# Three more weight buffers up to the first attention outputs, more halves split in advance, and another load order in the projection, in a one-layer encoder kernel

## The chip, the cores and the metric

The kernel runs on one core of one Trainium2 chip. The metric is the time of one execution on the device in microseconds (us). Where a distribution is given it is the median of the runs, with the lowest and the highest. One further execution was profiled; all views come from it.

## The reference

One layer of an encoder: attention over a window, then an MLP, each with a modulation by a conditioning vector c and a LayerNorm behind it. 256 tokens, width 2048, 32 query heads and 8 key heads of 64, hidden width 8192, everything in float32. Cut to its core:

```python
c_act = silu(c)                                            # 1 x 2048
sh_m, sc_m, g_m, sh_f, sc_f, g_f = split(c_act @ mod_w + mod_b, 6)   # mod_w: 2048 x 12288
h = x * (1 + sc_m) + sh_m                                  # 256 x 2048
q, k, v = split(h @ w_qkv + b_qkv)                         # 2048, 512, 512 columns; rotary on q and k
s = where(|qpos - kpos| <= 128, q k^T / 8, -inf)           # 4 query heads share a key head
m = max(max(s), sink)
p = exp(s - m) / (sum(exp(s - m)) + exp(sink - m))
x = layer_norm(ALPHA * x + (1 + g_m) * ((p v) @ w_o + b_o))
h = x * (1 + sc_f) + sh_f
x = layer_norm(ALPHA * x + (1 + g_f) * (relu(h @ w1 + b1) ** 2 @ w2 + b2))
```

The six modulation vectors need 100 MB of weights, as vector times matrix; w_qkv is 25 MB, w_o 17 MB, w1 and w2 67 MB each.

## The kernel before

**Precision.** A float32 product is made from rounded parts: each operand is split into a high part, rounded to fp32r, and a low part, the rest. Three matmuls (`mm3`: high by high, high by low, low by high) stand for one product. So every weight passes through ScalarE (the cast to `wh`, L234) and DVE (the difference `wl`, L206) before TensorE reads it in L472, L473 and L474.

**The weight stream.** All large weights come through one object, `Stream`, in blocks of 1 MB ([128 x 2048] float32). `plan` appends a block to the list `q`. `loads` (L188) issues the next block's DMA on SyncE's queue whenever one of the five buffers of the pool `raws` (`RAWS = 5`) is free; `self.free` counts them, in program order, and a buffer counts as free as soon as the instructions that read it have been issued. At run time the DMA waits until they have ended. A block has two kinds of use. A matmul block is split in two halves of 1024 columns: `pump` issues the cast of a half into a tile of the pool `whp` and `low` the difference into one of `wlp` (five tiles each); the buffer is counted free after the second half's difference. `S.nh` and `S.nl` say how many halves may be split ahead of the one in use (5 and 5 from the start, 4 and 2 from L604, 5 and 5 again from L835). A modulation block is used in whole, by `Mod.step`.

**Modulation.** `Mod.step` multiplies a block with c_act, either on TensorE (L292, small matmuls into the one bank of the pool `psm`) or, for the blocks that the set `dve` names, on DVE (L329, L331) into partial sums, which one more group of matmuls adds up at the end. `m_mix` are six groups of the attention's scale and shift (of 1, 1, 2, 4, 4, 4 column chunks of 128: `MIXG`), with 2 blocks for each chunk; `m_gm` is the attention's gate (16 blocks; blocks 5, 9, 12, 14 on DVE), `m_ff` the MLP's scale and shift, and `m_gf` the MLP's gate (all on DVE; its bias is added at its last step, L307 to L310).

**The projection.** Input group g is made by `modulated(g)`: the modulation's row is turned into columns, and ScalarE writes x times scale plus shift, rounded (L508), DVE the low part (L509, L510). Then `qkv(g, c)` multiplies chunk c of the group with its block of w_qkv (24 blocks in all, in the stream's order). A block of 4 column chunks has 48 matmuls into two PSUM banks; `evict` adds them into the sums `acc` on DVE (L526) where they aren't held in PSUM for the next block (`CARRY`). `ORDER` is the order of the chunks of a group. The lists in L409 to L425 say how the modulation blocks of group g + 1 lie between the w_qkv blocks of group g in the stream. The last six blocks of w_qkv (`LATE`: the query columns 3 to 5 of groups 4 and 5) come in the attention.

**The attention.** Keys and queries are rotated, split and turned (`split_k`, `split_q`, `heads_T` with its transposes in L677). A loop of 21 steps n (L856) overlaps the stages of 16 blocks of scores: `scores(n)` (L709, L710; exponentials on ScalarE in L723, with row sums), `normalise(n)` (L738), `probs_T(n - 1)` (transposes L748, copies L750), `values`, and between them one block of matmuls as filler: the six late blocks in steps 0 to 3, nothing in step 4, and from step 5 on the output projection `project` with w_o. `SLOT_FILL` says how many blocks of the gate and the MLP's modulation are planned in each step. In step 5 four tiles `ys` begin, at `gate` two more; the MLP takes `ys` anew, with two tiles for the second bias (`bias_all`).

**General tiles.** All other data of [128 x 1024] floats (x, group inputs, sums, keys, queries, probabilities, gate) lies in one pool, `gen`, of 26 tiles (`g4()`). A request for a tile waits until the oldest one that was given back is no longer read.

**Order.** The program is written in loops; a scheduler orders the instructions of each engine by their priority and by what they depend on. In the first part (`S.pin`) the casts, differences and modulation steps are kept in program order, and L508 to L510 always are.

Of the kernel before, what the change touches and what calls it, by code (L numbers as in the profile page):

```python
# [20 lines left out]
S = 256  # L21
# [16 lines left out]
         [(1, 0), (1, 1), (1, 3), (1, 2)]]  # L38
RAWS = 5
NHIGH = 5  # L40
NLOW = 5
# [4 lines left out]
def hybrid_kernel(ctx: ExitStack, tc: tile.TileContext, a, out: bass.AP):  # L46
# [5 lines left out]
    wlp = ctx.enter_context(tc.tile_pool(name="wlp", bufs=NLOW))  # L52
    gen = ctx.enter_context(tc.tile_pool(name="gen", bufs=26))
    psa = ctx.enter_context(tc.tile_pool(name="psa", bufs=5, space=PSUM))
    pst = ctx.enter_context(tc.tile_pool(name="pst", bufs=2, space=PSUM))
    psm = ctx.enter_context(tc.tile_pool(name="psm", bufs=1, space=PSUM))

    def g4(dt=F32):
# [101 lines left out]

    def bias_all(src):

        b = [g4(), g4()]
        for h in range(2):
            nc.gpsimd.dma_start(b[h], src[:, h * 1024:h * 1024 + 1024].partition_broadcast(128))
        return lambda c: b[c // 2][:, (c % 2) * 512:(c % 2) * 512 + 512]


    class Stream:
# [4 lines left out]
        def __init__(self):  # L174
            self.q, self.raw = [], []
            self.hs, self.ls, self.src = [], [], []
            self.free, self.used = RAWS, 0
            self.at = self.im = 0
            self.nh, self.nl = NHIGH, NLOW
            self.stop = 0  # L180
            self.pace = VECS
            self.pin = False
            self.side = {}
# [4 lines left out]
        def loads(self):  # L188
            while len(self.raw) < len(self.q) and self.free:
                if len(self.raw) in self.side:  # L190
                    self.side.pop(len(self.raw))()
                r = raws.tile([128, 2048], F32, name="raw")
                nc.sync.dma_start(r, self.q[len(self.raw)][0])
                self.raw.append(r)
                self.free -= 1

# [5 lines left out]
        def low(self):  # L202
            n = len(self.ls)
            r, kept = self.src[n]
            l = g4(F32R) if kept else wlp.tile([128, 1024], F32R, name="wl")
            self.pinned(nc.vector.tensor_sub(l, r, f32(self.hs[n])))  # L206
            self.ls.append(l)
            self.free += n % 2

        def pump(self, vecs, must=0):  # L210

            while len(self.ls) < must or self.at < len(self.q):
# [9 lines left out]
                if use is not None:  # L222
                    if not vecs and n >= must:
                        return
                    vecs = max(vecs - 1, 0)
                    use(self.raw[self.at])
                    self.at += 1
                    self.free += 1
                    continue
# [5 lines left out]
                self.hs.append(h)  # L235
                self.src.append((s, kept))
                self.at += n % 2

# [16 lines left out]
        def vecs(self, n):  # L255

            for _ in range(n):
                self.loads()
                if self.q[self.at][1] is None:
                    break  # L260
                self.q[self.at][1](self.raw[self.at])
                self.at += 1
                self.free += 1
            self.loads()
# [6 lines left out]
    class Mod:  # L271
# [26 lines left out]
        def step(self, raw):  # L298
# [7 lines left out]
            if last and self.whole:  # L306
                for n, p in enumerate(self.part):  # L307
                    b = g4()
                    nc.gpsimd.dma_start(b[0:1], self.bias[:, n * 1024:(n + 1) * 1024])
                    nc.gpsimd.tensor_add(p[0:1], p[0:1], b[0:1])  # L310
            elif i == self.n - 6 and self.bias is not None:
# [3 lines left out]
            for k in range(kc):  # L315
# [5 lines left out]
                elif i in self.dve:  # L321
                    e = min(4 * w, 1024)
                    new = self.part is None
                    if new:
                        self.part = [g4() for _ in range(4 * w // e)]
                    for n, p in enumerate(self.part):
# [39 lines left out]
    def gate(m):  # L366

        g = [g4(), g4()]
        src = [m.part[j // 2][:, (j % 2) * 512:(j % 2) * 512 + 512] for j in range(4)] if m.whole else [m.r]
# [42 lines left out]
    S.plan(a["wqkv"][1])  # L412
    S.plan(a["wqkv"][2])
    S.side[len(S.q)] = lambda: load_x(1)
    m_mix[2][0].plan(4)
    for g in range(2, G):
        n = len(ORDER[g])
        if g + 1 < G:
            S.side[len(S.q)] = lambda g=g: load_x(g)
        for x, c in enumerate(ORDER[g]):  # L420
            if g + 1 < G:
                m_mix[g + 1][0].plan([0, 0, 2][x] if g == 2 else [1, 2, 2, 1, 2, 0][x] if n == 6 else [3, 3, 2][x])
            wq(g, c)
        if g == 2:
            m_mix[3][0].plan(6)  # L425
    late = [m_gm] + [m[0] for m in m_ff[:3]]
# [176 lines left out]
    msk, pick = masks()  # L603
    S.nh, S.nl = 4, 2  # L604
    S.pace = 1
# [228 lines left out]

    S.nh, S.nl = NHIGH, NLOW  # L835
    kA = whole(rope(4, 0))
    khl = split_k(kA)
# [18 lines left out]
    for n in range(21):  # L856
# [10 lines left out]
        elif n < 5:  # L867
            w = iter((0, 1))
        else:
            if n == 5:  # L870
                ys = [g4() for _ in range(4)]
            w = project((n - 5) // 4, (n - 5) % 4)
# [165 lines left out]

    ys = [g4() for _ in range(4)]
    bf = bias_all(a["b2"])  # L1040
    for blk in range(BLK - 1):
# [140 lines left out]
```

## Time and profile before

| | |
|---|---|
| median of 3 runs | 1133.27 us (1132.55 to 1133.56) |
| profiled execution | 1132.9 us; its span in the profile 1131.2 us |
| TensorE's mean granted clock | 0.988 of full speed |
| TensorE matmuls (PE) | 1093.4 us busy, 97% of the span |
| TensorE weight loads (PEld) | 882.9 us, 78%, beside the matmuls |
| VectorE (DVE) | 808.9 us, 72% |
| ScalarE (ACT) | 545.9 us, 48% |
| GpSimd (POOL) | 28.9 us, 3% |
| DMA | 288.51 MB, mean 255 GB/s |

PE, PEld, DVE, ACT, POOL and SP (SyncE) are the engines. In the profile's forty slices each digit is an engine's busy share in tenths; PEclk is the clock that the throttle granted to TensorE. "L234" is line 234 of the kernel. A group's row has: line, engine, operation, output and input tiles, shapes and count, then busy time and mean ns of one, then the idle time of the engine ahead of these instructions and what ended most of it. A row of the timeline has: start, length, engine, line, operation, and in brackets the engine's idle time before it and what ended that. A row of the waits has: who waited, for what, then the total in us, the number of waits and the longest. A row of DMA issues ends with the median time from issue to landing.

The profile orders the chain of work that ended last by line: PE's L472, L473 and L474 (projections with mm3) have 17% each, L1012 (the MLP's first layer) 16%, DMA as a whole 3%, DVE 2%, ACT 1%.

### The profile page before, as it was taken

How to read it: one execution, taken by the hardware profiler on the slowest of the kernel's cores; microseconds unless marked ns; L12 is line 12 of the kernel's file. 1: busy time of each engine (PE TensorE's matmuls, PEld its weight loads, DVE VectorE, ACT ScalarE, POOL GpSimd, SP SyncE). 2: the span in 40 equal slices, each digit the busy share in tenths (PEclk: the TensorE clock that was granted, in tenths of full speed). 3: DMA queues.
4: the chain of work that ended last, by engine and by line, in shares of the span. 5: the costliest groups of instructions: out<-in, count | busy, mean ns of one | idle time of the engine just before them, and what ended most of it. 6: DMA issues, size and time to landing. Idle time of an engine off the chain costs nothing.

```text
span 1131.2 us, 15803 instructions
## 1 busy us (share of the span) xinstructions
PE 1093.4 (97%) x6258; PEld 882.9 (78%) x6258; DVE 808.9 (72%) x1122; ACT 545.9 (48%) x852; POOL 28.9 (3%) x48
## 2 busy tenths in 40 slices
PE   8779799999999999999999999999999999999995
PEld 6547576666676699998888888888888888888884
DVE  5477887877989977865568888866665656665576
ACT  6313255776676264753444543435444334444340
POOL 2000000000000000000000001020000000000001
PEclk9998999999999999999999999999999999999998
DMA  9799987867886699655577788874555557555521
GB/s 376 320 414 368 376 322 284 335 223 252 315 323 227 226 382 359 230 185 198 203 276 284 264 287 294 313 271 171 186 187 186 192 201 269 188 188 188 189 75 75
DMA packets 42882, 288.51 MB, mean 255 GB/s; under 512 B 5036, under 2 KB 5676, under 8 KB 9016
## 3 DMA queue, kind: packets, MB, share of 16 engines
q1 hardware_dynamic: 39824, 279.85, 67.1%
q0 software_dynamic: 2112, 6.32, 1.8%
q10 hardware_dynamic: 872, 1.34, 0.3%
q8 instruction: 49, 0.80, 0.3%
q14 instruction: 25, 0.20, 0.0%
HBM read 285.39 MB, written 2.10 MB: 254 GB/s over the span
## 4 chain that ended last, share of the span: by engine, by line
PE 93%; DMA 3%; DVE 2%; ACT 1%; issue 1%; DVEq 0%; ACTq 0%
PE pa L472 17%; PE pa L473 17%; PE pa L474 17%; PE pa L1012 16%; PE pa L1013 8%; PE pm L292 4%; PE pa L989 3%; PE pa L988 3%; PE pa L990 3%; DMA raw<-in_wqkv 2%; PE pa L763 2%; PE pt L748 1%; PE pa L709 1%; PE pt L677 1%; PE pa L710 1%; PE pa L590 1%
## 5 line engine op out<-in xcount | busy, mean ns | idle before, releaser
L206 DVE TENSOR_TENSOR wl<-raw,wh 128x1024 fp32r<-128x1024 f32 x332 | 405.6, 1227 | 230.7 <-ACT wh L234 230.2
L234 ACT CAST wh<-raw 128x1024 fp32r<-128x1024 f32 x332 | 347.9, 1053 | 451.7 <-PE pa L474 240.3
L472 PE MATMUL pa<-wh,g 128*128 128x512 f32 x816 | 322.7, 397 | 10.1 <-ACT g L508 8.8
L473 PE MATMUL pa<-wl,g 128*128 128x512 f32 x816 | 320.8, 394 | 1.2 <-DVE wl L206 1.2
L474 PE MATMUL pa<-wh,g 128*128 128x512 f32 x816 | 318.1, 392 | 0.0
L1012 PE MATMUL pa<-g,wh 128*128 128x512 f32 x768 | 271.6, 399 | 0.0
L1013 PE MATMUL pa<-g,wl 128*128 128x256 f32 x768 | 215.7, 281 | 0.0
L472 PEld LDWEIGHTS pa<-wh,g 128*128 128x128 f32 x816 | 154.6, 190 | 50.3 <-ACT g L508 10.8
L473 PEld LDWEIGHTS pa<-wl,g 128*128 128x128 f32 x816 | 154.6, 189 | 34.3 <-issue 1.8
L474 PEld LDWEIGHTS pa<-wh,g 128*128 128x128 f32 x816 | 153.9, 189 | 34.0 <-DVE g L510 0.9
L1012 PEld LDWEIGHTS pa<-g,wh 128*128 128x128 f32 x768 | 144.3, 188 | 35.8
L1013 PEld LDWEIGHTS pa<-g,wl 128*128 128x128 f32 x768 | 145.2, 189 | 0.2
L331 DVE SCALAR_TENSOR_TENSOR g<-raw,cact,g 128x1024 f32<-128x1024 f32 x81 | 103.2, 1279 | 8.0 <-DMA raw<-in_modgf 4.7
L989 PE MATMUL pa<-g,wh 128*128 128x256 f32 x256 | 72.7, 285 | 0.4 <-DVE g L932 0.4
L988 PE MATMUL pa<-g,wh 128*128 128x256 f32 x256 | 72.5, 286 | 0.0
L990 PE MATMUL pa<-g,wl 128*128 128x256 f32 x256 | 72.3, 283 | 0.0
L292 PE MATMUL pm<-raw,cact 128*32 128x256 f32 (+2 forms) x832 | 59.3, 381 | 10.3 <-DMA raw<-in_modm 9.2
L988 PEld LDWEIGHTS pa<-g,wh 128*128 128x128 f32 x256 | 48.8, 192 | 1.3 <-issue 0.8
L989 PEld LDWEIGHTS pa<-g,wh 128*128 128x128 f32 x256 | 49.1, 192 | 0.9 <-DVE g L932 0.8
L990 PEld LDWEIGHTS pa<-g,wl 128*128 128x128 f32 x256 | 49.1, 192 | 0.0
L292 PEld LDWEIGHTS pm<-raw,cact 128*32 128x32 f32 x832 | 22.7, 110 | 32.7 <-issue 11.4
L526 DVE TENSOR_TENSOR g<-g,pa 128x512 f32<-128x512 f32 x42 | 27.7, 681 | 17.4 <-PE pa L474 17.4
(178 smaller groups left out, 812.7 us busy)
## 6 DMA issues: line engine op xcount, KB each, us to landing
raw<-in_w SPq DMA_DIRECT2D x64, 1024.0 KB, 4.9
raw<-in_w1b SPq DMA_DIRECT2D x48, 1024.0 KB, 4.9
raw<-in_modm SPq DMA_DIRECT2D x32, 1024.0 KB, 8.1
raw<-in_modf SPq DMA_DIRECT2D x32, 1024.0 KB, 6.7
raw<-in_wqkv SPq DMA_DIRECT2D x24, 1024.0 KB, 8.1
raw<-in_modgm SPq DMA_DIRECT2D x16, 1024.0 KB, 5.8
raw<-in_wo SPq DMA_DIRECT2D x16, 1024.0 KB, 7.0
raw<-in_w1a SPq DMA_DIRECT2D x16, 1024.0 KB, 6.7
```

The source lines that it names most:

```text
L206: self.pinned(nc.vector.tensor_sub(l, r, f32(self.hs[n])))
L234: self.pinned(nc.scalar.copy(h, s))
L292: i = nc.tensor.matmul(self.ps[32 * j:32 * j + 32, :w], lhsT[j] if type(lhsT) is list else lhsT, rhs[j], start=self.first, stop=stop)
L331: nc.vector.scalar_tensor_tensor(p[:, :e], s, cact[:, kt:kt + 1], p[:, :e], op0=OP.mult, op1=OP.add)
L472: nc.tensor.matmul(ps, xh, wh, start=start, stop=False)
L473: nc.tensor.matmul(ps, xh, wl, start=False, stop=False)
L474: nc.tensor.matmul(ps, xl, wh, start=False, stop=stop)
L988: nc.tensor.matmul(o, wh(w, 128), hh, start=new, stop=False)
L989: nc.tensor.matmul(o, wh(w, 128), hl, start=False, stop=False)
L990: nc.tensor.matmul(o, wl(w, 128), hh, start=False, stop=end)
L1012: nc.tensor.matmul(ps, wh(k, 128), hb, start=k == 0, stop=False)
L1013: nc.tensor.matmul(ps[:, :256], wl(k, 128), hb[:, :256], start=False, stop=k == NK - 1)
```

## The change

- **Buffers.** A second pool, `raws2`, of three 1 MB buffers (`MORE = 3`) stands beside the five of `raws`. `self.free` becomes a list of pools from which `loads` takes the next buffer; `home` remembers where each block lies, and `freed` returns its buffer. From the line after the projection's loop on (`S.deep = False`), buffers of `raws2` are no longer returned.
- **General tiles.** The pool `gen` has 20 tiles instead of 26. The room of `raws2` is given at its first use after that to six tiles `g4b`: `ys` (from step n = 5), the gate's tiles, the MLP's `ys` and its second bias, and the partial sums of the MLP's gate.
- **Halves.** `S.nh, S.nl` are 5, 4 instead of 4, 2 in the projection.
- **Order of loads.** In the projection the last modulation block of group 2 comes after the first w_qkv block of that group; the first w_qkv block of each later group comes at the end of the group before it, one block ahead of the last modulation block for group 3; the modulation blocks lie otherwise between the w_qkv blocks. Blocks and bytes in all are the same.
- **The MLP gate's bias** is loaded and added in four pieces of 512 in the small tiles `t2` instead of two pieces of 1024 in general tiles.

```diff
--- before.py
+++ after.py
@@ -37,6 +37,7 @@
          [(0, 4), (0, 5), (1, 4), (1, 5)],
          [(1, 0), (1, 1), (1, 3), (1, 2)]]
 RAWS = 5
+MORE = 3
 NHIGH = 5
 NLOW = 5
 VECS = 2
@@ -50,10 +51,22 @@
     raws = ctx.enter_context(tc.tile_pool(name="raws", bufs=RAWS))
     whp = ctx.enter_context(tc.tile_pool(name="whp", bufs=NHIGH))
     wlp = ctx.enter_context(tc.tile_pool(name="wlp", bufs=NLOW))
-    gen = ctx.enter_context(tc.tile_pool(name="gen", bufs=26))
+    gen = ctx.enter_context(tc.tile_pool(name="gen", bufs=20))
     psa = ctx.enter_context(tc.tile_pool(name="psa", bufs=5, space=PSUM))
     pst = ctx.enter_context(tc.tile_pool(name="pst", bufs=2, space=PSUM))
     psm = ctx.enter_context(tc.tile_pool(name="psm", bufs=1, space=PSUM))
+
+
+    early = ExitStack()
+    ctx.push(early.__exit__)
+    raws2 = early.enter_context(tc.tile_pool(name="raws2", bufs=MORE))
+    more = []
+
+    def g4b(dt=F32):
+        if not more:
+            early.close()
+            more.append(ctx.enter_context(tc.tile_pool(name="gen2", bufs=2 * MORE)))
+        return more[0].tile([128, 1024], dt, tag="g4b", name="g4b")
 
     def g4(dt=F32):
         return gen.tile([128, 1024], dt, tag="g4", name="g4")
@@ -158,7 +171,7 @@
 
         return add
 
-    def bias_all(src):
+    def bias_all(src, g4=g4):
 
         b = [g4(), g4()]
         for h in range(2):
@@ -174,7 +187,9 @@
         def __init__(self):
             self.q, self.raw = [], []
             self.hs, self.ls, self.src = [], [], []
-            self.free, self.used = RAWS, 0
+            self.free, self.home, self.used = [raws] * RAWS + [raws2] * MORE, [], 0
+            self.of = []
+            self.deep = True
             self.at = self.im = 0
             self.nh, self.nl = NHIGH, NLOW
             self.stop = 0
@@ -189,10 +204,14 @@
             while len(self.raw) < len(self.q) and self.free:
                 if len(self.raw) in self.side:
                     self.side.pop(len(self.raw))()
-                r = raws.tile([128, 2048], F32, name="raw")
+                self.home.append(self.free.pop(0))
+                r = self.home[-1].tile([128, 2048], F32, name="raw")
                 nc.sync.dma_start(r, self.q[len(self.raw)][0])
                 self.raw.append(r)
-                self.free -= 1
+
+        def freed(self, n):
+            if self.deep or self.home[n] is raws:
+                self.free.append(self.home[n])
 
         def pinned(self, i):
 
@@ -205,7 +224,8 @@
             l = g4(F32R) if kept else wlp.tile([128, 1024], F32R, name="wl")
             self.pinned(nc.vector.tensor_sub(l, r, f32(self.hs[n])))
             self.ls.append(l)
-            self.free += n % 2
+            if n % 2:
+                self.freed(self.of[n])
 
         def pump(self, vecs, must=0):
 
@@ -225,7 +245,7 @@
                     vecs = max(vecs - 1, 0)
                     use(self.raw[self.at])
                     self.at += 1
-                    self.free += 1
+                    self.freed(self.at - 1)
                     continue
                 if n >= must and (n - self.used >= self.nh or kept):
                     return
@@ -234,6 +254,7 @@
                 self.pinned(nc.scalar.copy(h, s))
                 self.hs.append(h)
                 self.src.append((s, kept))
+                self.of.append(self.at)
                 self.at += n % 2
 
         def main(self):
@@ -260,7 +281,7 @@
                     break
                 self.q[self.at][1](self.raw[self.at])
                 self.at += 1
-                self.free += 1
+                self.freed(self.at - 1)
             self.loads()
 
     S = Stream()
@@ -304,10 +325,11 @@
             last = self.i == self.n
             per = 1024 // w
             if last and self.whole:
-                for n, p in enumerate(self.part):
-                    b = g4()
-                    nc.gpsimd.dma_start(b[0:1], self.bias[:, n * 1024:(n + 1) * 1024])
-                    nc.gpsimd.tensor_add(p[0:1], p[0:1], b[0:1])
+                for n in range(4):
+                    b, p = sml.tile([128, 512], F32, name="br", tag="t2", bufs=4), self.part[n // 2]
+                    p = p[0:1, n % 2 * 512:n % 2 * 512 + 512]
+                    nc.gpsimd.dma_start(b[0:1], self.bias[:, n * 512:n * 512 + 512])
+                    nc.gpsimd.tensor_add(p, p, b[0:1])
             elif i == self.n - 6 and self.bias is not None:
                 self.br = [sml.tile([128, 512], F32, name="br", tag="t2", bufs=4) for _ in range(4)]
                 for n, b in enumerate(self.br):
@@ -322,7 +344,7 @@
                     e = min(4 * w, 1024)
                     new = self.part is None
                     if new:
-                        self.part = [g4() for _ in range(4 * w // e)]
+                        self.part = [(g4b if self.whole else g4)() for _ in range(4 * w // e)]
                     for n, p in enumerate(self.part):
                         s = raw[:, k * 4 * w + n * e:k * 4 * w + n * e + e]
                         if new:
@@ -365,7 +387,7 @@
 
     def gate(m):
 
-        g = [g4(), g4()]
+        g = [g4b(), g4b()]
         src = [m.part[j // 2][:, (j % 2) * 512:(j % 2) * 512 + 512] for j in range(4)] if m.whole else [m.r]
         hl = [g4(F32R) for _ in src]
         for p, v in zip(hl, src):
@@ -411,18 +433,25 @@
     m_mix[1][0].plan(2)
     S.plan(a["wqkv"][1])
     S.plan(a["wqkv"][2])
+
     S.side[len(S.q)] = lambda: load_x(1)
-    m_mix[2][0].plan(4)
+    m_mix[2][0].plan(3)
+    wq(2, 1)
+    m_mix[2][0].plan(1)
     for g in range(2, G):
         n = len(ORDER[g])
         if g + 1 < G:
             S.side[len(S.q)] = lambda g=g: load_x(g)
-        for x, c in enumerate(ORDER[g]):
+        for x, c in enumerate(ORDER[g][1:], 1):
             if g + 1 < G:
-                m_mix[g + 1][0].plan([0, 0, 2][x] if g == 2 else [1, 2, 2, 1, 2, 0][x] if n == 6 else [3, 3, 2][x])
+                m_mix[g + 1][0].plan([0, 0, 3][x] if g == 2 else [0, 2, 2, 2, 1, 1][x] if n == 6 else [0, 4, 4][x])
             wq(g, c)
         if g == 2:
-            m_mix[3][0].plan(6)
+            m_mix[3][0].plan(4)
+        if g + 1 < G:
+            wq(g + 1, ORDER[g + 1][0])
+        if g == 2:
+            m_mix[3][0].plan(1)
     late = [m_gm] + [m[0] for m in m_ff[:3]]
     lp = [0]
 
@@ -601,7 +630,7 @@
     modulated(0)
     idle(6)
     msk, pick = masks()
-    S.nh, S.nl = 4, 2
+    S.nh, S.nl = 5, 4
     S.pace = 1
     run(qkv_first(0))
     S.vecs(2)
@@ -833,6 +862,7 @@
 
 
     S.nh, S.nl = NHIGH, NLOW
+    S.deep = False
     kA = whole(rope(4, 0))
     khl = split_k(kA)
     run(qkv(G - 1, 1))
@@ -868,7 +898,7 @@
             w = iter((0, 1))
         else:
             if n == 5:
-                ys = [g4() for _ in range(4)]
+                ys = [g4b() for _ in range(4)]
             w = project((n - 5) // 4, (n - 5) % 4)
         S.vecs(SLOT_FILL.get(n, 0) if len(LATE) - 2 <= n < 5 else 0)
         mid = mids(n)
@@ -1036,8 +1066,8 @@
                 S.done()
         return pss
 
-    ys = [g4() for _ in range(4)]
-    bf = bias_all(a["b2"])
+    ys = [g4b() for _ in range(4)]
+    bf = bias_all(a["b2"], g4b)
     for blk in range(BLK - 1):
         if blk:
             us = ff_hidden(blk)
```

## The prediction

> **What bounds the kernel now.** I read the page's forty slices first. Each slice is 28.3 us.
>
> ```profile
> span 1131.2 us, 15803 instructions
> ...
> PE   8779799999999999999999999999999999999995
> ...
> PEclk9998999999999999999999999999999999999998
> DMA  9799987867886699655577788874555557555521
> GB/s 376 320 414 368 376 322 284 335 223 252 315 323 227 226 382 359 230 185 198 203 276 284 264 287 294 313 271 171 186 187 186 192 201 269 188 188 188 189 75 75
> ```
>
> TensorE is full from slice 6 on. Only the first five slices, the projection, have gaps, and there the loads run at 320 to 414 GB/s. So the change works where time can be had, and anything that opens a gap later costs its whole length. The windows of 5 us through the projection and the sums of waits name the gaps (columns: length, then busy us and instructions of PE, PE's weight loads, DVE, ACT and POOL, then granted clock, DMA share, GB/s):
>
> ```profile
> 35.00:40.00 5.00, 2.01 (x8) 1.03 (x9) 1.43 (x6) 1.55 (x2) 0.00 (x0) 0.93 1.02 429
> 40.00:45.00 5.00, 5.00 (x17) 4.04 (x18) 0.91 (x1) 2.57 (x5) 0.00 (x0) 0.72 1.01 418
> 45.00:50.00 5.00, 5.00 (x23) 3.88 (x21) 4.64 (x7) 3.02 (x5) 0.00 (x0) 1.00 0.17 70
> 50.00:55.00 5.00, 4.90 (x35) 3.31 (x35) 5.00 (x8) 2.04 (x3) 0.00 (x0) 1.00 0.59 195
> 75.00:80.00 5.00, 0.69 (x16) 0.13 (x4) 1.84 (x2) 1.99 (x2) 0.00 (x0) 1.00 1.01 428
> 80.00:85.00 5.00, 1.94 (x16) 0.60 (x16) 2.47 (x3) 0.53 (x1) 0.00 (x0) 0.53 1.03 434
> 85.00:90.00 5.00, 3.92 (x9) 3.14 (x10) 4.41 (x8) 4.39 (x8) 0.00 (x0) 0.50 1.00 419
> 105.00:110.00 5.00, 5.00 (x42) 3.61 (x40) 2.32 (x3) 0.00 (x0) 0.00 (x0) 1.00 0.99 341
> 130.00:135.00 5.00, 0.95 (x13) 0.43 (x6) 1.29 (x2) 1.93 (x3) 0.00 (x0) 0.99 0.97 408
> 135.00:140.00 5.00, 5.00 (x16) 3.95 (x15) 4.97 (x10) 2.99 (x6) 0.00 (x0) 0.67 1.02 431
> ...
> ACT wh L234 <- DMA raw<-in_wqkv: 33.7, 7, 9.8
> ```
>
> There are three gaps, near 37, from 75 to 85 and near 132, each followed by a stretch at a lowered clock. In each the loads run at 408 to 434 GB/s, but before it they did not: 70 and 195 GB/s from 45 to 55, 341 at 105. The stream had stopped, because all five raw buffers were held by blocks that TensorE or DVE had not used up; then it ran late. The last row says who waits: ScalarE's cast of a weight half. The timeline (start, length, instruction) shows why that stops TensorE:
>
> ```profile
> 28.63 1.08 PE L292 MATMUL pm<-raw,cact 128*32 128x128 f32 x32 [0.34 <-DMA raw<-in_modm]
> 33.56 1.08 PE L292 MATMUL pm<-raw,cact 128*32 128x128 f32 x32 [0.53 <-DMA raw<-in_modm]
> 40.98 0.33 SPq L193 DMA_DIRECT2D raw<-in_wqkv  x1
> 51.15 11.97 SPq L193 DMA_DIRECT2D raw<-in_modm  x6
> 84.47 1.04 ACT L234 CAST wh<-raw 128x1024 fp32r<-128x1024 f32 x1 [5.40 <-DMA raw<-in_wqkv]
> 85.43 2.07 ACT L508 ACTIVATE g<-g,shm,scm 128x256 fp32r<-128x256 f32 x4
> 86.08 0.79 PE L472 MATMUL pa<-wh,g 128*128 128x512 f32 x1 [2.22 <-ACT g L508]
> 133.07 1.04 ACT L234 CAST wh<-raw 128x1024 fp32r<-128x1024 f32 x1 [9.85 <-DMA raw<-in_wqkv]
> 134.02 2.07 ACT L508 ACTIVATE g<-g,shm,scm 128x256 fp32r<-128x256 f32 x4
> 134.67 0.61 PE L472 MATMUL pa<-wh,g 128*128 128x512 f32 x1 [4.05 <-ACT g L508]
> ...
> 180.94 0.80 PE L677 MATMUL pt<-identr,g 128*128 128x128 f32 x8
> ```
>
> L508 makes a group's input. It stands on ScalarE behind a cast of a later weight block (the eighth wqkv block for group 3, the fourteenth for group 4), so TensorE waits until that block lands. Nothing was issued between 40.98 and 51.15. The last row is the first transpose of the keys, by which the attention's start can be dated.
>
> **The change, part by part.** I sum against the profiled execution, 1132.9 us (span 1131.2 and 1.7 around it), 0.4 under the median of the three runs, 1133.27.
>
> *Three more buffers and the new order.* Modulation blocks 5 and 7 (counted from 0) were used at 28.63 and 33.56: two blocks in 4.93 us, so one per 2.47 us while the queue is full. Block 5 ends the first 9.25 MB of the stream, so MB number m lands at 5.8 + 2.47 m as long as the queue never empties. By the loads in order of issue, the eighth wqkv block ended 28.25 MB before and ends 27.25 now; the fourteenth 45.75 and now 43.75. The rule gives 75.6 and 118.8 for before; the trace has 84.5 and 133.1, so the empty queue cost 8.9 us by the second gap and 14.3 by the third. In the changed program each load's wait is on an earlier release; following those through the first 115 us, I find 3.5 to 6 blocks always under way, so I let the rule hold:
>
> Group 3: the eighth block lands at 5.8 + 2.47 x 27.25 = 73.1. In the new order both of its halves are cast ahead of L508 (2 x 1.05), L508's first takes 0.6: TensorE starts at 75.8 instead of 86.08. Group 4: the fourteenth lands at 113.9, and with the same 2.7 TensorE starts at 116.6 instead of 134.67. That is 18.1 us.
>
> Is another engine late then? From 75.8 TensorE has 144 matmuls and five modulation blocks (1.07 each, L292 above). Twelve matmuls of one half run like this:
>
> ```profile
> 210.80 0.40 PE L472 MATMUL pa<-wh,g 128*128 128x512 f32 x1
> 213.32 0.39 PE L474 MATMUL pa<-wh,g 128*128 128x512 f32 x1
> ...
> L206 DVE TENSOR_TENSOR wl<-raw,wh 128x1024 fp32r<-128x1024 f32 x332 | 405.6, 1227 | 230.7 <-ACT wh L234 230.2
> L331 DVE SCALAR_TENSOR_TENSOR g<-raw,cact,g 128x1024 f32<-128x1024 f32 x81 | 103.2, 1279 | 8.0 <-DMA raw<-in_modgf 4.7
> L526 DVE TENSOR_TENSOR g<-g,pa 128x512 f32<-128x512 f32 x42 | 27.7, 681 | 17.4 <-PE pa L474 17.4
> ```
>
> Eleven starts in 2.52 us, 0.229 each: 144 x 0.229 = 33.0, with 5.3 for the blocks and 1.6 for transposes it is free at 115.7. DVE has in that stretch 12 low halves (12 x 1.23 = 14.7), 12 modulation steps (15.3), 12 evictions (8.2) and some 2 small: 40.2 us of 40.8. So DMA, DVE and TensorE are all within a microsecond or two of being the bound, and no lost time is taken up again. TensorE also gains the slow stretch after the third gap ((1 - 0.67) x 5 = 1.7) and owes one modulation block more (1.1). 18.1 + 1.7 - 1.1 = 18.7; for the tight balance I take 17 (bounds 8, if half of the queue's lost time stays, and 20). After group 4 TensorE is the bound in both, with the same work up to the attention.
>
> *More halves split in advance (nh 5, nl 4).* This puts a second cast in front of L508, 1.05 us at each group; it is in the sum. What stands behind the waiting cast on ScalarE is L508 itself, and TensorE behind that.
>
> *Six of the 26 general tiles gone until output 5.* The attention's start has to live with 20: the x columns (4), four projected columns, two modulated groups in two halves (4), keys (4), queries (2) and two bias tiles fill them. The exponentials of score block 1 then get a tile only when group 4's input is done with. The instruction order of the changed kernel shows it: on ScalarE L723 of block 1 now stands behind casts that wait for wqkv block 22's matmuls, and TensorE runs blocks 22 and 23 (48 matmuls) in one go before the transposes of block 1, where the kernel before spread them between the transposes. That filler is missing afterwards. Before, block 2's scores to the first output projection took this, with TensorE dense:
>
> ```profile
> 209.74 0.39 PE L709 MATMUL pa<-g,g 128*128 128x256 f32 x1
> 238.83 0.50 PE L472 MATMUL pa<-wh,g 128*128 128x512 f32 x1
> ...
> 214.70 0.47 ACT L723 ACTIVATE g<-pa,nm 128x256 f32<-128x256 f32 x1
> ...
> 216.60 1.08 ACT L750 COPY g<-pt 128x512 f32<-128x512 f32 x2
> 217.54 1.74 ACT L738 ACTIVATE g<-g,rs 128x256 f32<-128x256 f32 x4
> ...
> raw<-in_w SPq DMA_DIRECT2D x64, 1024.0 KB, 4.9
> ...
> raw<-in_modgm SPq DMA_DIRECT2D x16, 1024.0 KB, 5.8
> ```
>
> 29.1 us. In the new order I count from those scores: the filler is used up at 14.9, its one wait for a PSUM bank (a 0.68 eviction) included. ScalarE then does block 1's exponentials (1.8), a cast, the copies (1.08), and its normalising (1.74) to 19.8; block 2 the same to 25.3; TensorE has followed with transposes and gate block 13 at 26.6. Now gate block 15 stands next in line (before, it came after two output blocks). Its load waits for a raw buffer that DVE frees only after the row sums of block 3 (28.4) and one more modulation step (29.7); it lands 4.9 (a load without a queue ahead of it, as in the two DMA rows, where the gate's own took 5.8) later, near 34.6. After it come its closing matmuls (1), the copy of block 2 (36.6, its tile was the gate's partial sum), the query transposes with their copies (39), the scores, and the first output matmul when DVE and ScalarE have freed a bank, near 43. Of these 43 us, 2.6 is work that came later before (block 15 and its closing). Loss 43 - 29.1 - 2.6 = 11.3; I take 11.5. Bounds: 4, if block 15 lands in time and only the chain of exponentials shows, and 20, if the wait for block 14 and the cooled clock add up.
>
> *Rest.* The gate, output and b2 tiles move to the six tiles that take the buffers' room; they are written after the stream has left those buffers. The gate's bias comes in four pieces on GpSimd, beside second-layer matmuls. Both at nothing; if that cover goes, some 2 us.
>
> Sum: 1132.9 - 17 + 11.5 = 1127.4. Against the median, 1127.8; I say 1127.5.
>
> **A rule of the skill.** The windows show 408 to 434 GB/s in a full queue. The Trainium skill, DMA: Bandwidth & Descriptors, section Bandwidth, under "Where 436 GB/s comes from", says that for transfers from HBM to SBUF the HBM side binds, at some 358 GB/s a core. By that one block takes an estimated 2.93 us, group 4 starts near 131, and the sum comes to some 1140 by estimate. The trace differs: seven of the windows above are over that figure, at 408 to 434.
>
> **The rivals.** *The attention is covered.* Tiles come free earlier than I count, or gate block 15 does: loss 4, so 1132.9 - 17 + 4 = 1119.9. For it: before, nothing in that stretch waited long. Against: the order is fixed, and TensorE cannot pass block 15.
>
> *Slower: releases hold the stream.* In group 3's stretch DVE, 40.2 us of work in 40.8, frees a raw buffer with each second low half. If it falls behind by some 9 us the queue runs low again, as at 105 (341 GB/s), and the fourteenth block lands near 123: gain 8.5, loss 11.5, 1135.9. It decides once group 4 starts later than about 122, where gain and loss are even.
>
> *The full rate is not kept.* The stream full from 40 to 115 has not been seen; the longest full stretch shown lasted 15 us. If it kept only the 341 GB/s of the window at 105, a block would take 1.0486 MB / 341 = 3.07 us. From the block that the rule lands at 37.3 (m = 12.75) it is 31 blocks to the fourteenth: 37.3 + 31 x 3.07 = 132.5, group 4 at 135.2, no gain there, 1132.9 + 11.5 = 1144. The window at 105 held a stopped queue, though, not a slow one.
>
> **How the numbers follow.** Forecast 0.52 (its own range 1122 to 1132), covered attention 0.22, late releases 0.20, lower rate 0.06. What a measurement of this kernel tells from no change is 0.2%, 2.3 us. Of the forecast 0.46 lies below 1131, 0.06 within; covered attention is all faster; late releases 0.04 within and 0.16 above; the lower rate slower. Faster 0.68, same 0.10, slower 0.22. The range 1117 to 1138 leaves out part of the second case and the last.
>
> **What would show it.** Right: no DMA window under 300 GB/s between 40 and 115; L472 of group 3 near 76 and of group 4 near 117; the first L677 near 163 instead of 181; then, after blocks 22 and 23 in one go, a hole of some 8 us in TensorE in front of a gate block, and 40 us or more from block 2's scores to the first output. The output projection and both MLP layers shifted, not stretched. Wrong: a third gap as long as before, or no hole in the attention.

## The result and the profile after

The changed kernel takes 1150.53 us (median of 4 runs, 1147.50 to 1150.89) against 1133.41 before: a ratio of 1.0142, 95% interval 1.0120 to 1.0165. The forecast was 1127.5 with a range of 1117 to 1138. The kernel is slower by 17 us, where 6 less were forecast.

The profiled execution took 1150.79 us. The span, TensorE's row, the granted clock and the transfers of its page:

```profile
span 1149.0 us, 15814 instructions
...
PE   8899999689999999999999998999999999999994
...
PEclk9999999879999999999999999999999999999997
...
GB/s 377 424 426 425 428 268 268 314 78 209 308 337 246 252 384 337 199 184 187 229 279 260 289 285 302 267 245 143 187 184 187 200 199 183 184 184 260 204 49 73
```

The projection is now full: 424 to 428 GB/s in slices 2 to 5, and from 40 us to the attention TensorE waits nowhere longer than 2.62 us. But slices 8 and 9 have a new hole with a lowered clock, the stream falls to 78 GB/s behind it, and slice 25 has another dent. Windows of the changed kernel, first those of the old gaps (columns as in the prediction), then the new ones:

```profile
45.00:50.00 5.00, 5.00 (x45) 3.04 (x46) 4.76 (x8) 2.04 (x3) 0.00 (x0) 1.00 1.02 428
50.00:55.00 5.00, 5.00 (x22) 4.12 (x23) 5.00 (x8) 2.11 (x2) 0.00 (x0) 1.00 1.00 421
80.00:85.00 5.00, 5.00 (x24) 4.14 (x23) 4.96 (x5) 2.00 (x2) 0.00 (x0) 1.00 1.02 428
130.00:135.00 5.00, 5.00 (x24) 4.02 (x23) 4.16 (x5) 3.49 (x4) 0.00 (x0) 1.00 1.02 429
225.00:230.00 5.00, 0.00 (x0) 0.00 (x0) 0.00 (x0) 0.79 (x2) 0.00 (x0) 0.50 0.94 385
240.00:245.00 5.00, 5.00 (x26) 3.64 (x21) 0.85 (x3) 1.86 (x4) 0.00 (x0) 0.50 0.07 29
700.00:705.00 5.00, 1.44 (x7) 0.86 (x5) 5.00 (x7) 1.06 (x1) 0.54 (x1) 1.00 0.77 261
775.00:780.00 5.00, 2.48 (x15) 1.88 (x13) 2.75 (x3) 2.03 (x3) 0.00 (x0) 1.00 0.51 169
```

The timeline rows that answer to those of the prediction (L254 is the cast, L537 the group's input, L501 to L503 the three matmuls, L706 the transposes, L738 the scores; the last row is the first output projection):

```profile
73.39 1.99 ACT L254 CAST wh<-raw 128x1024 fp32r<-128x1024 f32 x2 [6.31 <-DMA raw<-in_wqkv]
75.94 0.49 PE L501 MATMUL pa<-wh,g 128*128 128x512 f32 x1 [2.62 <-ACT g L537]
113.91 2.00 ACT L254 CAST wh<-raw 128x1024 fp32r<-128x1024 f32 x2 [5.75 <-DMA raw<-in_wqkv]
116.46 0.50 PE L501 MATMUL pa<-wh,g 128*128 128x512 f32 x1
165.23 0.80 PE L706 MATMUL pt<-identr,g 128*128 128x128 f32 x8
193.69 0.39 PE L738 MATMUL pa<-g,g 128*128 128x256 f32 x1
248.44 0.50 PE L501 MATMUL pa<-wh,g 128*128 128x512 f32 x1
```

Set against before, from the same rows and others of the two timelines, the difference grows so:

| mark | before | after | difference |
|---|---|---|---|
| group 3's first matmul | 86.08 | 75.94 | -10.1 |
| group 4's first matmul | 134.67 | 116.46 | -18.2 |
| scores of block 2 | 209.74 | 193.69 | -16.05 |
| first output projection | 238.83 | 248.44 | +9.6 |
| first matmul of the MLP | 396.76 | 400.79 | +4.0 |
| block 1's first eviction in the MLP's second layer | 700.53 | 705.24 | +4.7 |
| block 2's first eviction there | 875.78 | 888.93 | +13.15 |
| TensorE's last matmul ends | 1119.02 | 1132.83 | +13.8 |
| span | 1131.2 | 1149.0 | +17.8 |

So four terms: the projection gains 16.05; the attention loses 20.1 (4.03 + 16.05); the MLP's second layer loses 9.1 (13.15 - 4.03); the end loses 4.65 (17.8 - 13.15). The forecast had 17, 11.5, nothing and nothing.

**The attention's hole**, in the changed kernel's timeline:

```profile
204.07 1.05 ACT L254 CAST wh<-raw 128x1024 fp32r<-128x1024 f32 x1 [5.27 <-PE pa L503]
206.44 0.46 ACT L752 ACTIVATE g<-pa,nm 128x256 f32<-128x256 f32 x1
221.27 1.94 PE L313 MATMUL pm<-raw,cact 128*32 128x512 f32 x8 [1.66 <-DMA raw<-in_modgm]
223.25 1.01 SPq L209 DMA_DIRECT2D raw<-in_modgm  x2
230.45 2.48 DVE L353 SCALAR_TENSOR_TENSOR g<-raw,cact,g 128x1024 f32<-128x1024 f32 x2 [6.46 <-DMA raw<-in_modgm]
232.91 1.93 PE L313 MATMUL pm<-raw,cact 128*32 128x512 f32 x8 [9.71 <-DMA raw<-in_modgm]
236.59 1.07 ACT L779 COPY g<-pt 128x512 f32<-128x512 f32 x2 [10.80 <-PE pm L313]
```

Block 1's exponentials (L752) run only at 206.44, behind casts (204.07) that wait for the matmuls of wqkv blocks 22 and 23, as the instruction order had shown. TensorE then reaches gate block 15 with nothing else to do; gate blocks 14 and 15 are issued together at 223.25, and 15 has landed at 232.91. The copy of block 2 (L779) waits for the gate's sum to end, since it needs its tile.

**The MLP.** The source line of block 0's evictions in the changed kernel, then the same line in the kernel before, then rows of the changed kernel's timeline (L351 is the first write of a partial sum of the MLP's gate).

```profile
L1081 DVE TENSOR_TENSOR g4b<-pa,g4b x8: 680/682/685, 522.1 to 783.9; 128x512 f32<-128x512 f32 x8
```

```profile
L1051 DVE TENSOR_TENSOR g<-pa,g x8: 680/682/684, 518.1 to 584.0; 128x512 f32<-128x512 f32 x8
```

```profile
566.84 0.74 DVE L351 TENSOR_SCALAR g4b<-raw,cact 128x1024 f32<-128x1024 f32 x1
568.63 0.74 DVE L351 TENSOR_SCALAR g4b<-raw,cact 128x1024 f32<-128x1024 f32 x1
705.98 0.79 PE L501 MATMUL pa<-wh,g 128*128 128x512 f32 x1 [4.53 <-DVE g4b L1083]
780.09 0.50 PE L1042 MATMUL pa<-g,wh 128*128 128x512 f32 x1 [2.61 <-DVE rl L991]
```

The last of the eight evictions of block 0 began at 584.0 before. After, six are done by 567, the two partial sums are first written right behind them, and the last two evictions, column 3, come at 783. Until then their two of the five PSUM banks are held, and TensorE waits twice (4.53 and 2.61 us) for an instruction of DVE that empties another bank.

**The end.** DVE's evictions of the last two output tiles, before and after (L771 and L800 are the same line), and the last halves' casts after:

```profile
1108.17 0.69 DVE L771 TENSOR_TENSOR tmp<-pa,g 128x512 f32<-128x512 f32 x1 [7.69 <-PE pa L474]
1119.05 0.69 DVE L771 TENSOR_TENSOR tmp<-pa,g 128x512 f32<-128x512 f32 x1 [2.14 <-PE pa L474]
```

```profile
1124.36 1.05 ACT L254 CAST g<-raw 128x1024 fp32r<-128x1024 f32 x1 [3.34 <-PE pa L503]
1128.54 0.69 DVE L800 TENSOR_TENSOR tmp<-pa,g4b 128x512 f32<-128x512 f32 x1 [1.51 <-PE pa L503]
1134.05 0.68 DVE L800 TENSOR_TENSOR tmp<-pa,g4b 128x512 f32<-128x512 f32 x1
1137.65 0.68 DVE L801 TENSOR_TENSOR g<-g,tmp 128x512 f32<-128x512 f32 x1
```

Before, 10.9 us lay between them and the first token half's normalising fitted in. After, 5.5: the cast of a last half came at 1124.36, and the second half's sum waits on DVE until 1137.65. From the end of TensorE's last matmul to the end of the span it is 16.2 us, where it was 12.2 before.

### The profile page after: what moved, and what is told of

Read it like the earlier page. It is cut to its first block, busy times and chain, and to the rows that moved or that the text cites. A ratio compares the mean times of both kernels' runs of the same rounds, so it can differ in the third digit from the quotient of the medians.

```text
span 1149.0 us, 15814 instructions
## 1 busy us (share of the span) xinstructions
PE 1097.7 (96%) x6258; PEld 883.1 (77%) x6258; DVE 812.1 (71%) x1122; ACT 546.8 (48%) x852; POOL 32.8 (3%) x52
## 4 chain that ended last, share of the span: by engine, by line
PE 82%; DMA 7%; DVE 6%; ACT 3%; issue 2%; POOL 0%; DVEq 0%; SPq 0%; ACTq 0%; POOLq 0%
PE pa L1042 15%; PE pa L501 14%; PE pa L503 14%; PE pa L502 14%; PE pa L1043 8%; PE pm L313 4%; DMA raw<-in_modm 3%; PE pa L1019 3%; PE pa L1018 3%; PE pa L1020 3%; DVE wl L225 2%; PE pa L792 1%; DMA raw<-in_wqkv 1%; PE pt L777 1%; ACT wh L254 1%
## 5 line engine op out<-in xcount | busy, mean ns | idle before, releaser
L254 ACT CAST wh<-raw 128x1024 fp32r<-128x1024 f32 x332 | 347.7, 1053 | 462.4 <-PE pa L503 242.5
L501 PE MATMUL pa<-wh,g 128*128 128x512 f32 x816 | 322.0, 396 | 10.2 <-DVE g4b L1083 4.5
L503 PE MATMUL pa<-wh,g 128*128 128x512 f32 x816 | 318.7, 392 | 1.4 <-DVE g L539 1.4
L501 PEld LDWEIGHTS pa<-wh,g 128*128 128x128 f32 x816 | 153.5, 188 | 50.7 <-DVE g4b L1083 5.0
L503 PEld LDWEIGHTS pa<-wh,g 128*128 128x128 f32 x816 | 153.4, 188 | 38.5 <-DVE g L539 3.6
L353 DVE SCALAR_TENSOR_TENSOR g<-raw,cact,g 128x1024 f32<-128x1024 f32 x51 | 65.1, 1278 | 6.9 <-DMA raw<-in_modgm 6.5
L353 DVE SCALAR_TENSOR_TENSOR g4b<-raw,cact,g4b 128x1024 f32<-128x1024 f32 x30 | 38.0, 1279 | 2.6 <-DMA raw<-in_modgf 2.5
## 6 DMA issues: line engine op xcount, KB each, us to landing
raw<-in_modm SPq DMA_DIRECT2D x32, 1024.0 KB, 15.6
```

Source lines behind the costliest of these rows:

```text
L254: self.pinned(nc.scalar.copy(h, s))
L353: nc.vector.scalar_tensor_tensor(p[:, :e], s, cact[:, kt:kt + 1], p[:, :e], op0=OP.mult, op1=OP.add)
L501: nc.tensor.matmul(ps, xh, wh, start=start, stop=False)
L503: nc.tensor.matmul(ps, xl, wh, start=False, stop=stop)
```

## The experiments

The theory after the comparison: all three losses come from the tiles, that is from the split of 26 general tiles into 20 and six that only certain data may use. Its rivals: the shifted stream or the new order makes the attention's hole; the gate bias in four pieces makes the MLP's waits; the end is chance. In the verdicts a ratio is to the kernel before, run beside it.

**Order and halves alone.** Before, with the new list of loads and

```diff
-    S.nh, S.nl = 4, 2
+    S.nh, S.nl = 5, 4
```

> The kernel before with only the new order of loads and the halves 5 and 4 instead of 4 and 2 in the projection; five buffers and 26 general tiles stay. Theory (the loss of the changed kernel comes from the six general tiles it gave away): the attention, the MLP and the tail are as before, 29 us from block 2's scores to the first output projection and no hole; the projection gains a part, since L508 waits for blocks that stand 1 to 2 MB earlier in the stream (2.5 to 5 us), more if the queue then runs dry less: 1124 to 1130. Rival (the earlier start of the attention, with the stream in another phase, makes the hole): with half of the gain the hole is there too, 1138 or more. Second rival (buffers alone bring the gain): 1133, no change.

1128.05 us, ratio 0.9951 (0.9934 to 0.9968), as the theory had it. By the trace the scores of block 2 come 4.04 us earlier and the first matmul of the MLP 4.2: no hole. The stream still runs low (216 GB/s from 50 to 55, where the changed kernel has 421).

**The tiles alone.** The changed kernel, old order, halves 4 and 2, and

```diff
-            self.free, self.home, self.used = [raws] * RAWS + [raws2] * MORE, [], 0
+            self.free, self.home, self.used = [raws] * RAWS, [], 0
```

> The changed kernel with the old order of loads, halves 4 and 2, and the three extra buffers never used: their room lies idle until it becomes the six other tiles. So only the tiles and the four bias pieces differ from before. Theory (tiles): the projection as before (group 4's first matmul near 135), then the whole loss at its three places: 20.1 in the attention, 9.1 in the MLP's second layer between blocks 0 and 2, 4.6 at the end: 1133.4 + 33.8 = 1167. Rival (the stream's other phase or the new order makes the loss): 1133 to 1137.

1170.03 us, ratio 1.0315 (1.0292 to 1.0339). The loss is there without the new order and without a deeper stream: 18.1 us in the attention, and 15.6 from there to the end of the span (37.9 - 22.3). The 4.2 us by which block 2's scores come later than before were not foreseen; what in the projection makes them wasn't followed up.

**Room for the sums.** The changed kernel and

```diff
     ys = [g4b() for _ in range(4)]
+    for y in ys:
+        nc.gpsimd.memset(y[0:1, 0:1], 0.0)
     bf = bias_all(a["b2"], g4b)
```

> The changed kernel, with one element of each of the MLP's four sum tiles ys written by GpSimd when they are requested, so that each holds its room from then on. Theory (the partial sums of the MLP's gate took the room of the fourth sum tile, so two of the five PSUM banks waited with column 3 of block 0 from 587 to 783 us): column 3 of block 0 is evicted near 587, both waits of TensorE in the MLP (4.5 and 2.6 us, 9.1 with what follows) go, 1150.5 - 9.1 = 1141.4. Rival (the gate's bias in four pieces on GpSimd makes these waits, through the small tiles that it shares with the LayerNorm's rows): 1150, no change.

1140.93 us, ratio 1.0067 (1.0052 to 1.0082): 9.6 less than the changed kernel, 0.5 beside the forecast, with the four bias pieces untouched. The source line of block 0's evictions (L1083 in this kernel) and the window of the first wait:

```profile
L1083 DVE TENSOR_TENSOR g4b<-pa,g4b x8: 681/682/684, 521.4 to 587.3; 128x512 f32<-128x512 f32 x8
```

```profile
700.00:705.00 5.00, 5.00 (x24) 4.14 (x23) 5.00 (x7) 1.67 (x3) 1.03 (x2) 1.00 0.77 262
```

All eight are done at 588 again, and TensorE is full where it had 1.44 of 5 us; from 775 to 780 it has 4.89. The second partial sum is now first written at 588.02, behind column 3, where it came at 568.63. From the first matmul of the MLP to TensorE's last one it takes 723.0 us (changed kernel 732.0, before 722.3). The attention's hole stays (first matmul of the MLP at 400.09). So the partial sums of the MLP's gate had taken the room of the fourth sum tile, whose first write is that eviction, until the gate was built at 783. The bias pieces don't make these waits.

**Early use of the six tiles.** The changed kernel and

```diff
-        P = g4()
+        P = g4b() if n < 4 else g4()
...
-        pT = g4()
+        pT = g4b() if n < 4 else g4()
```

> The changed kernel, where the probabilities and their transposes of blocks 0 to 3 take the six other tiles, which lie idle until output 5. Theory (a shortage of tiles up to output 5 makes the hole in the attention): block 1's exponentials come before wqkv blocks 22 and 23 again, block 2's scores to the first output projection take 29 to 33 us instead of 54.7, 1150.5 - 20 = 1130, or 1135 if a part of the shortage stays. Rival (the hole is the late gate block 15, whose load waits for a raw buffer): the hole stays at 10 us or more, 1140 to 1150.

1137.71 us, ratio 1.0028 (1.0013 to 1.0042): 12.8 of the 20 are back, fewer than forecast. Block 1's exponentials and the window of the hole:

```profile
201.21 0.47 ACT L752 ACTIVATE g4b<-pa,nm 128x256 f32<-128x256 f32 x1 [1.41 <-DVE nm L746]
```

```profile
225.00:230.00 5.00, 5.00 (x25) 2.31 (x22) 2.82 (x8) 3.09 (x13) 0.00 (x0) 1.00 0.36 136
```

They start at 201.21 instead of 206.44, the wqkv blocks lie between the transposes again, and TensorE is full. From block 2's scores (194.75) to the first output projection it now takes 32.7 us (227.41), within the 29 to 33 expected. From the scores to the first matmul of the MLP 6.6 us are still lost. Two waits that the kernel before doesn't have, of 0.89 and 0.74 us near 217 and 219, are a part of it; what makes the rest stays open.

**The last halves.** The changed kernel; the halves of the last block that are kept to the end take the other tiles. The value planned here is now the function that a kept half gets its tile from; the two lines that use it are not shown:

```diff
-                S.plan(a["w2"][blk, c, kg], None, blk == BLK - 1 and c == 3 and kg > 1)
+                S.plan(a["w2"][blk, c, kg], None, blk == BLK - 1 and c == 3 and (None, None, g4, g4b)[kg])
```

> The changed kernel, where the last weight block's four halves (high and low), which are kept to the end, take four of the six other tiles instead of general ones. Theory (they waited for general tiles while the other tiles of the used-up sums lay idle, so the last two output tiles end 6 us apart instead of 11 and DVE has both to do): the order of before returns at the end, the span after TensorE's last matmul is 12.2 us instead of 16.2 and the matmuls end 0.6 earlier: 1150.5 - 4.6 = 1146. Rival (the tail is long because all came later, or by chance of this profile): 1150, no change.

1146.29 us, ratio 1.0113 (1.0084 to 1.0141), 4.2 less. The interval overlaps that of the changed kernel, 1.0120 to 1.0165, so the times alone don't show the gain. The trace does: the casts of kept halves come early, one at 1098.49, and DVE's two evictions lie 10.9 us apart again:

```profile
1098.49 1.05 ACT L254 CAST g4b<-raw 128x1024 fp32r<-128x1024 f32 x1
1118.82 0.69 DVE L800 TENSOR_TENSOR tmp<-pa,g4b 128x512 f32<-128x512 f32 x1 [7.69 <-PE pa L503]
1129.70 0.69 DVE L800 TENSOR_TENSOR tmp<-pa,g4b 128x512 f32<-128x512 f32 x1 [2.13 <-PE pa L503]
```

From the end of TensorE's last matmul to the end of the span it is 12.1 us. In the traces of the four kernels that keep these halves in 20 general tiles (the changed kernel, the tiles alone, room for the sums, early tiles) it is 16.2 to 16.3, and in those of all the others 12.1 to 12.2. So the long end is not chance.

**All three edits**, and the same with the old order and halves:

> The changed kernel with the three edits together: early tiles for the probabilities of blocks 0 to 3, held room for the sums, and the other tiles for the last halves. Theory (three separate shortages of tiles, on three stretches that don't overlap): the gains add up, 1150.5 - 12.8 - 9.6 - 4.6 = 1123.5, and the projection's 16 us stay. Rival (one hides the other, or the edits compete for the same six tiles): 1129 or more. Both the kernel before and the order alone (1128) are beaten if the theory holds.

> The kernel with the three edits, but with the old order of loads and halves 4 and 2: the eight buffers by themselves, free of the tiles' costs. Theory (the queue runs dry for want of buffers, and the buffers bring most of the gain; the order alone brought 5.5): group 4's first matmul near 122 to 125 instead of 134.7, 1127 to 1131. Rival (buffers and order only work together, since L508 still waits for a block that stands 2 MB later): group 4 near 130 or later, 1133 to 1137.

1125.06 us, ratio 0.9922 (0.9900 to 0.9945), and 1124.06, ratio 0.9919 (0.9898 to 0.9940). The gains add up within 1.6 us. The second expectation missed on the good side: the eight buffers without the new order and halves bring as much as with them. In the traces block 2's scores come 14.2 us early with the new order and 13.5 with the old, although group 4's first matmul is 3.7 us later with the old (121.96 against 118.24).

**Two buffers and one**, instead of three, with 22 and 24 general tiles. With two, the four other tiles serve early probabilities, sums and last halves; the two other tiles of the third kernel serve early probabilities, gates, bias and the gate's partial sums. The second kernel has two buffers with the old order and halves. The first lines of the edit for two:

```diff
-MORE = 3
+MORE = 2
...
-    gen = ctx.enter_context(tc.tile_pool(name="gen", bufs=20))
+    gen = ctx.enter_context(tc.tile_pool(name="gen", bufs=22))
```

> The kernel with the three edits, but two more buffers instead of three, 22 general tiles and four other tiles, which hold the early probabilities, the sums and the last halves; gate, bias and partial sums are in general tiles. Theory (the queue is full with 3.5 blocks or more under way, and the eighth buffer is the margin): the projection gains 12 to 16, the attention loses a little less: 1121 to 1126. Rival (DVE, with 40 us of work in 41, frees the buffers too late, and the eighth buffer is needed): the queue runs dry again, group 4 near 123 or later, 1128 to 1132.

> The kernel with two more buffers and the three edits, but with the old order of loads and halves 4 and 2. Theory (the buffers bring the gain, the order adds next to nothing once the queue is full, as with three buffers, where group 5 came 0.6 us later by the old order): 1116 to 1119. Rival (with seven buffers the queue is at its margin, and the old order makes it run dry): group 4's first matmul later than 125, 1121 to 1127.

> The changed kernel with one more buffer instead of three: 24 general tiles and two other tiles for the probabilities of blocks 0 to 3, the gates, the second bias and the gate's partial sums; sums and last halves in general tiles. Theory (each buffer brings a part until the queue never runs dry, which with two it does not): between the order alone (1128) and two buffers (1117), 1119 to 1124, with DMA below 400 GB/s somewhere between 40 and 115 us. Rival (one more buffer is enough): 1117 to 1119 and the queue full up to 140. Second rival (the tiles, 24 and two, cost in the attention again): a hole there, 1125 or more.

| kernel | median us | ratio (interval) | scores of block 2 | first matmul of the MLP |
|---|---|---|---|---|
| two, new order | 1116.72 | 0.9870 (0.9822 to 0.9917) | -15.2 | -16.7 |
| two, old order | 1121.34 | 0.9887 (0.9864 to 0.9910) | -11.1 | -12.45 |
| one, new order | 1122.16 | 0.9888 (0.9865 to 0.9911) | -11.6 | -11.5 |

Two buffers did better than the 1121 to 1126 expected and have the lowest median of all, below both given kernels, though the interval overlaps those of the other two rows: 15.2 of the projection's 16.05 us are there, and nothing is lost in the attention (window of that kernel):

```profile
215.00:240.00 25.00, 25.00 (x130) 16.52 (x130) 19.92 (x40) 18.34 (x51) 0.00 (x0) 1.00 0.55 202
```

The windows from 60 to 65 of two buffers, new order, then old order, then of one buffer, show that the stream runs low in the other two:

```profile
60.00:65.00 5.00, 4.83 (x26) 3.81 (x25) 5.00 (x7) 1.84 (x2) 0.00 (x0) 1.00 1.01 415
```

```profile
60.00:65.00 5.00, 5.00 (x34) 3.48 (x33) 5.00 (x7) 0.83 (x2) 0.00 (x0) 1.00 1.02 347
```

```profile
60.00:65.00 5.00, 5.00 (x36) 3.77 (x36) 5.00 (x7) 2.98 (x4) 0.00 (x0) 1.00 0.69 256
```

The old order with two missed its 1116 to 1119 and came out at the rival's time, though group 4's first matmul, at 123.87, is not as late as the rival had it; one buffer came out as its theory said. With seven buffers in all the old order lets the stream run low, with six the new one does. So order and buffers stand in for each other: the new order, with its halves, counts at five (the first experiment, 4 us) and seven (4 us by the traces; the intervals of the two overlap), not at eight.

**The halves alone.** Before, with 5 and 4:

> The kernel before with halves 5 and 4 instead of 4 and 2 in the projection, and nothing else. Theory (more halves split early free raw buffers earlier, since a buffer is free after the second half's difference, at the price of one more cast in front of L508): between 1130 and 1134. Rival (the halves alone make the 5.5 us that halves and order together brought): 1128. Second rival (the second cast in front of L508 costs its 1.05 us at three groups): 1136.

1136.17 us, ratio 1.0006 (0.9991 to 1.0020): no difference that can be measured. The 5.5 us of the first experiment are not the halves' alone. No run has the new order with the old halves.

## Why the prediction was wrong

**Right: the stream and the projection.** The rule 5.8 + 2.47 m gave 73.1 and 113.9 for the two blocks; their casts start at 73.39 and 113.91. TensorE starts groups 3 and 4 at 75.94 and 116.46, forecast 75.8 and 116.6. No window of 5 us from 40 to 115 is under 417 GB/s. The keys' first transpose comes at 165.23, where 163 was told, and the term came to 16.05 us where 17 was taken. Where the Trainium skill's figure of 358 GB/s was weighed, the rows have 421 to 429. The Trainium skill, HBM Reference, section Specifications (TRN2), says that a core that streams alone gets some 425; the trace agrees with that figure.

**Right in kind, too small: the attention.** The term "Loss 43 - 29.1 - 2.6 = 11.3" measured 20.1, just past its upper bound of 20. All events came in the order told, and the load of gate block 15 was issued 29.6 us after the scores (forecast 29.7). Two steps were mis-sized. "It lands 4.9 later": two blocks were issued together and block 15 took 9.7. And from the landing to the first output I had 8.4 us of work at full clock; it took 15.5. TensorE came out of the hole at half clock and kept it for 12.3 us (last section), which by an estimate makes up at most half of that, 6.2 of the 7.1 us. So the first output came 54.75 us after the scores instead of 43; 5.6 us were made up behind it, where I had 2.6. The early tiles confirm the cause for 13.5 of the 20.1 (6.6 are left), and the kernels with 22 or 24 general tiles lose nothing there.

**Wrong: "Rest. Both at nothing."** This is the step that failed. I counted how many tiles each stage holds up to output 5, and took the six others as equal to general ones from then on. They are not: only sums, gates, the second bias and the gate's partial sums may lie in them. With four sums and two bias tiles they are full, and the two partial sums claim room in the order in which tiles are first written, ahead of the fourth sum. That cost 9.1 us, and the last halves, which may not lie there, 4.65. For each an edit that changes nothing else takes the cost away: the sums' room by the time and the trace, the last halves by the trace. The sign "The output projection and both MLP layers shifted, not stretched" failed with that step. Of the rivals none had a cost after output 5; "releases hold the stream" had a slower kernel, but for another reason, since the stream never ran low in the projection.

With these two costs in place of nothing the sum would have been 1132.9 - 17 + 11.5 + 9.1 + 4.65 = 1141, outside the range by this step alone; the rest up to 1150.8 is 8.6 of the attention and 1 of the projection.

## What to carry to other kernels

When buffers are paid for with working tiles, count the tiles for every later stage up to the last, by pool and not in all, and look at the built order for a write that waits for room: here an eviction that was the first write of its tile came at 784 instead of 584 and held two PSUM banks for nearly 200 us. A deeper queue pays only until the transfer rate is full, here at seven buffers with the new order; with the eighth block 2's scores came no earlier (14.2 us against 15.2), and it takes two more general tiles. Compare marks along the whole kernel, since a large gain at the start was hidden here by three losses behind it.

## What the runs showed of the hardware

How long TensorE kept the lowered clock differed between two places. Two more windows of the changed kernel, behind the attention's hole and behind the MLP's first wait:

```profile
245.00:250.00 5.00, 5.00 (x24) 2.96 (x22) 3.96 (x13) 2.99 (x12) 0.00 (x0) 0.98 0.00 0
705.00:710.00 5.00, 4.03 (x11) 3.20 (x12) 5.00 (x7) 1.05 (x1) 0.54 (x1) 0.66 0.94 292
```

After the wait of 4.5 us that ended at 705.98, half the clock lasted (1 - 0.66) x 5 / 0.5 = 3.4 us of dense matmuls. After the attention's hole TensorE resumed at 232.91 with modulation matmuls of 32 columns, bias matmuls of one row and transposes, and had half the clock up to 245.2, for 12.3 us, although its row shows no idle time in between. The first matmul of the scores in that stretch began at 241.91, 3.3 us before the clock came back. The Trainium skill, TensorE: Matmul & The Clock Gate, section What's actually happening, says that some 3.4 us of sustained work bring the clock back. The MLP's wait agrees with it; the attention's hole does not, if the small matmuls count as work, and no run here shows whether they do.
